# ReLU and row sum on one core: who clears the semaphores, how the last four rows are cut into loads, and which wait the last sum carries

## The chip, the cores and the metric

The kernel runs on 1 core of one Trainium2 chip. The metric is the device time of one execution in microseconds (us). On one core every run below was fast (granted clock 1.0 in each), so all of them can be compared. "Faster" and "slower" mean more than 2% with a 95% interval clear of it.

## The reference

```python
batch, seq, dim = 32, 512, 1024          # float32, normal random numbers
def reference(x):
    relu_x = np.maximum(x, 0)
    return np.sum(relu_x, axis=-1).astype(np.float32)
```

That is 16,384 rows of 1024 numbers: 67.11 MB in, 0.07 MB out, each byte read once.

## The kernel before

The rows lie over 128 partitions, 128 rows in each. Seven loads of 16 rows per partition (8 MB each) go through three buffers, and the last 16 rows come in shrinking loads. Most rows are clamped by ScalarE and summed by VectorE. Near the end each engine does whole rows alone, one instruction per row, whose accumulator then gives the sum. SyncE issues every load and store. Instruction order and semaphores are written by hand: each load has its own semaphore, which counts to 16 when it has landed (the trace has 16 increments of each); `act` and `dve` count finished instructions of ScalarE and VectorE; `stored` counts stores.

```python
TAIL = [8, 4, 2, 1]                  # rows per load at the end
PIECES = [244, 252, 260, 268]        # the last row, in four loads by columns
# ...
    for part, w in zip(parts, PIECES):
        arrived.append(load(part[:, :w], rows(m, 1)[:, 0, col : col + w]))
        col += w
    store(0, ROWS, *freed[0])
    store(ROWS, NT - ROWS - 2, n_act - 1, n_dve)

    last, w = parts[-1], PIECES[-1]
    for i in range(extra):           # the first three pieces; each sum becomes a column of the fourth
        dve_row(parts[i][:, :], last[:, w + i : w + i + 1], arrived[i])
    nc.vector.wait_ge(arrived[-1], 16)
    before_last = n_dve
    nc.vector.tensor_scalar(         # the last sum: 268 columns and three partial sums
        # ...
        accum_out=res[:, NT - 1 : NT],
    ).wait_op(sems.dve, before_last, "sem-ge").then_inc(sems.dve, 1)
    n_dve += 1
    store(NT - 2, 2, n_act, n_dve)   # the last store, two columns
    nc.sync.sem_inc(sems.issued, 1)
# ... and after the body:
    nc.sync.wait_ge(sems.stored, 16 * n_stores).then_inc(sems.stored, -16 * n_stores)
    # ...
    nc.gpsimd.wait_ge(sems.issued, 1)
    nc.gpsimd.drain(semaphore_range=cleared)
    nc.gpsimd.sem_clear(cleared)     # all semaphores back to 0 for the next execution
```

In the traces no instruction carries more than one wait (51 carry one in the kernel before). For the last sum, which needs two, one of them is an instruction of its own on VectorE's queue (21 ns).

Of the kernel before, what the change touches and what calls it, by code (L numbers as in the profile page):

```python
# [4 lines left out]
F32 = mybir.dt.float32  # L5
RELU = mybir.ActivationFunctionType.Relu
MAX, ADD = mybir.AluOpType.max, mybir.AluOpType.add
P = 128

ROWS = 16  # L10
# [3 lines left out]
TWO = [[16], [16], [16], [8, 8], [8, 8], [7, 7], []]  # L14
ACT = [0, 0, 0, 0, 0, 2, 9]
DVE = [0, 0, 0, 0, 0, 0, 7]

TAIL = [8, 4, 2, 1]
PIECES = [244, 252, 260, 268]

EARLY = 1

# [1 line left out]
def kernel(tc: tile.TileContext, x: bass.AP, out: bass.AP):  # L24
    nc = tc.nc
    sems = Semaphores(tc)

    tc.close()
    tc.compile()
    nc.cur_bb = nc.bb_map[tc.start_bb_name]  # L30
    body = nc.cur_bb.bb.instructions
    ends = list(body)
    body.clear()
    n_stores = relu_sum(nc, sems, x, out)
    body.extend(ends)


    nc.cur_bb = nc.bb_map[tc.start_bb_name + "_end"]
    nc.cur_bb.bb.instructions.clear()
    nc.sync.wait_ge(sems.stored, 16 * n_stores).then_inc(sems.stored, -16 * n_stores)  # L40
    nums = sorted(s.num for s in (*sems.loads, sems.act, sems.dve, sems.issued))
    cleared = range(nums[0], nums[-1] + 1)
    assert len(cleared) == len(nums)
    nc.gpsimd.wait_ge(sems.issued, 1)
    nc.gpsimd.drain(semaphore_range=cleared)
    nc.gpsimd.sem_clear(cleared)
    issue_ahead_of_the_barrier(tc, EARLY)


class Semaphores:  # L50
    def __init__(self, tc: tile.TileContext):
        n = len(TWO) + len(TAIL) + len(PIECES)
        self.loads = [tc.alloc_semaphore(f"load{i}") for i in range(n)]
        self.act = tc.alloc_semaphore("act")
        self.dve = tc.alloc_semaphore("dve")
        self.issued = tc.alloc_semaphore("issued")
        self.stored = tc.alloc_semaphore("stored")


def relu_sum(nc, sems: Semaphores, x: bass.AP, out: bass.AP):  # L60
    x_flat = x.flatten_outer_dims()
    N, D = x_flat.shape
    NT = N // P
    NB = len(TWO)
    assert N == P * NT == P * ROWS * (NB + 1)
    assert sum(TAIL) == ROWS - 1 and sum(PIECES) == D

    bufs = [nc.alloc_sbuf_tensor(f"io{i}", [P, ROWS, D], F32) for i in range(NBUF)]
    res = nc.alloc_sbuf_tensor("res", [P, NT], F32)
    extra = len(PIECES) - 1  # L70
    parts = [
        nc.alloc_sbuf_tensor(f"piece{i}", [P, w + extra * (i == extra)], F32)
        for i, w in enumerate(PIECES)
    ]


# [7 lines left out]
    def rows(m, n):  # L84
        if m < ROWS:
            return xf[:, m : m + n, :]
        return xv[:, m - ROWS : m - ROWS + n, :]

    def sums(m, n):
        if m < ROWS:  # L90
            return of[:, m : m + n], res[:, m : m + n]
        return ov[:, m - ROWS : m - ROWS + n], res[:, m : m + n]
# [3 lines left out]
    def load(dst, src, after=None):  # L96
        nonlocal n_load
        dma = nc.sync.dma_start(out=dst, in_=src)  # L98
        if after:
            dma.wait_op(sems.dve, after[1], "sem-ge")  # L100
        dma.then_inc(sems.loads[n_load], 16)
        n_load += 1
        return sems.loads[n_load - 1]

    def store(m, n, act, dve):
        nonlocal n_store
        dst, src = sums(m, n)
        nc.sync.wait_ge(sems.act, act)
        nc.sync.dma_start(out=dst, in_=src).wait_op(sems.dve, dve, "sem-ge").then_inc(
            sems.stored, 16  # L110
        )
        n_store += 1
# [16 lines left out]
    def act_row(ap, m, loaded):  # L129
        nonlocal n_act  # L130
        i = nc.scalar.activation(  # L131
            out=ap, in_=ap, func=RELU, accum_out=res[:, m : m + 1]
        )
        if loaded is not None:
            i.wait_op(loaded, 16, "sem-ge")
        i.then_inc(sems.act, 1)
        n_act += 1

    def dve_row(ap, accum_out, loaded):
        nonlocal n_dve  # L140
        i = nc.vector.tensor_scalar(  # L141
            out=ap,
            in0=ap,
            scalar1=0.0,
            scalar2=None,
            op0=MAX,
            op1=ADD,
            accum_out=accum_out,
        )
        if loaded is not None:  # L150
            i.wait_op(loaded, 16, "sem-ge")
        i.then_inc(sems.dve, 1)
        n_dve += 1

    freed = []
    m = 0
    for j in range(NB):
        buf = bufs[j % NBUF]
        loaded = load(buf[:, :, :], rows(m, ROWS), j >= NBUF and freed[j - NBUF])
        c = 0  # L160
# [19 lines left out]
    buf = bufs[NB % NBUF]  # L180
    c = 0
    for n in TAIL:
        loaded = load(
            buf[:, c : c + n, :], rows(m, n), None if c else freed[NB - NBUF]
        )
        for i in range(n):
# [3 lines left out]
                dve_row(buf[:, c, :], res[:, m : m + 1], loaded if i == 1 else None)  # L190
            c += 1
            m += 1
    col = 0
    arrived = []
    for part, w in zip(parts, PIECES):
        arrived.append(load(part[:, :w], rows(m, 1)[:, 0, col : col + w]))
        col += w



    store(0, ROWS, *freed[0])
    store(ROWS, NT - ROWS - 2, n_act - 1, n_dve)

    last, w = parts[-1], PIECES[-1]
    for i in range(extra):
        dve_row(parts[i][:, :], last[:, w + i : w + i + 1], arrived[i])
    nc.vector.wait_ge(arrived[-1], 16)
    before_last = n_dve
    nc.vector.tensor_scalar(  # L209
        out=last[:, :],  # L210
        in0=last[:, :],
# [1 line left out]
        scalar2=None,  # L213
        op0=MAX,
        op1=ADD,
        accum_out=res[:, NT - 1 : NT],
    ).wait_op(sems.dve, before_last, "sem-ge").then_inc(sems.dve, 1)
    n_dve += 1
    store(NT - 2, 2, n_act, n_dve)
    nc.sync.sem_inc(sems.issued, 1)  # L220
    return n_store


def issue_ahead_of_the_barrier(tc: tile.TileContext, n_loads: int):


    SP = mybir.EngineType.SP
    blocks = tc.nc.main_func.blocks
    opening = blocks[0].instructions
    body = next(b for b in blocks if b.name == tc.start_bb_name).instructions  # L230
    loads = [i for i in body if i.engine == SP][:n_loads]
    for i in loads:
        assert isinstance(i, mybir.InstDMACopy)
        body.remove(i)
    at = next(
        n
        for n, i in enumerate(opening)
        if i.engine == SP and isinstance(i, mybir.InstDrain)
    )
    opening[at:at] = loads  # L240
# [30 lines left out]
```

## Time and profile before

| | kernel before |
|---|---|
| time, median of 6 runs | 161.30 us (161.13 to 161.50) |
| span of the profiled run (first to last instruction) | 160.0 us |
| DMA queue, share of the span | 98.0% |
| VectorE, ScalarE busy | 74%, 65% |
| last load landed | 157.97 us |
| last sum, start to end | 158.11 to 158.55 us |
| end of the last store | 159.97 us |

The prediction below shows the lines for the queue, the chain that ended last and the last sums. Two more matter. In such lines DVE is VectorE, ACT is ScalarE, POOL is GpSimd and SP is SyncE; a q marks work of the engine's instruction queue, and L40 is line 40 of the kernel. The first is from the list of SyncE's waits (who waited for whom, us in total, times, longest); L40 is its wait for the stores:

```profile
SPq L40 <- SPq L40: 1.0, 1, 1.0
```

The second is GpSimd's clear of the semaphore range (duration in ns, least, median and most, then first and last start in us):

```profile
L46 POOLq EVENT_SEMAPHORE_RANGE_CLEAR  x1: 136/136/136, 159.1 to 159.1; - x1
```

It was over at 159.25, while SyncE stood waiting for the store until 159.99.

The stages of the tail are tenths of a microsecond. So I also use the trace's landing records (the moment at which the sixteenth count of a load's semaphore arrives) and its instruction starts, in thousandths of a microsecond.

### The profile page before, as it was taken

To read this page: it belongs to the slowest core of one execution; us is meant where nothing else is said; L and a number is where in the kernel's file an instruction comes from. 1 tells how busy PE (TensorE), PEld (TensorE's weight loads), DVE (VectorE), ACT (ScalarE), POOL (GpSimd) and SP (SyncE) were. 2 spreads that over 40 slices of the span, in tenths; PEclk is the share of its full clock that TensorE was granted. 3 is DMA by queue.
4 is the path that set the end of the run, shared out by engine and by line. 5 is a ranking of instruction groups with operands and counts; after the bars stand their busy time and mean duration, and the time that the engine had idled before them with its cause. 6 is when DMAs were issued, how large, how long until landed. Compare 5 with 4: busy or idle time off the path is not lost.

```text
span 160.0 us, 135 instructions
## 1 busy us (share of the span) xinstructions
DVE 117.7 (74%) x43; ACT 104.2 (65%) x50; POOL 0.2 (0%) x4
## 2 busy tenths in 40 slices
DVE  0000000009999499994999999999999999999995
ACT  3000049990699808996099951999339992499993
POOL 0000000000000000000000000000000000000000
DMA  7996996996996997999979969969969969898993
GB/s 262 524 508 279 524 492 295 524 491 295 524 491 295 524 442 344 524 393 393 524 344 442 524 262 524 524 262 524 524 262 524 491 295 524 377 410 385 428 405 109
DMA packets 2592, 67.18 MB, mean 420 GB/s; under 512 B 672, under 2 KB 1184, under 8 KB 1312
## 3 DMA queue, kind: packets, MB, share of 16 engines
q1 hardware_dynamic: 2592, 67.18, 98.0%
HBM read 67.11 MB, written 0.07 MB: 420 GB/s over the span
## 4 chain that ended last, share of the span: by engine, by line
DMA 43%; DVE 33%; ACT 17%; another core or an unknown queue 3%; SPq 1%; issue 0%
DVE res L124 32%; DMA io<-in_x_dram 25%; DMA piece<-in_x_dram 18%; ACT io L116 17%; SPq L98 1%; DVE piece L141 1%; DVE piece L209 0%
## 5 line engine op out<-in xcount | busy, mean ns | idle before, releaser
L124 DVE TENSOR_REDUCE res<-io 128x8 f32<-128x8192 f32 (+2 forms) x9 | 101.1, 11291 | 40.2 <-ACT io L116 40.2
L116 ACT ACTIVATE io<-io 128x8192 f32<-128x8192 f32 (+2 forms) x9 | 81.7, 9111 | 47.2 <-DMA io<-in_x_dram 47.2
L131 ACT ACTIVATE io<-io 128x1024 f32<-128x1024 f32 x20 | 20.9, 1045 | 5.4 <-DMA io<-in_x_dram 5.3
L141 DVE TENSOR_SCALAR_CACHE_REDUCE io<-io 128x1024 f32<-128x1024 f32 x13 | 15.1, 1225 | 0.2
L131 ACT ACTIVATION_READ_ACCUMULATOR io<-io 128x1 f32 x20 | 3.7, 187 | 0.0
L116 ACT ACT_TABLE_LOAD x1 | 1.3, 1283 | 0.8 <-PEq L255 0.8
L141 DVE TENSOR_SCALAR_CACHE_REDUCE piece<-piece 128x244 f32<-128x244 f32 (+2 forms) x3 | 1.2, 415 | 0.5 <-DMA piece<-in_x_dram 0.5
L141 DVE DVE_READ_ACCUMULATOR io<-io 128x1 f32 x13 | 1.2, 93 | 0.0
L209 DVE TENSOR_SCALAR_CACHE_REDUCE piece<-piece 128x271 f32<-128x271 f32 x1 | 0.4, 435 | 0.0
L141 DVE DVE_READ_ACCUMULATOR piece<-piece 128x1 f32 x3 | 0.2, 83 | 0.0
L255 POOL MEMSET const-bfloat16-1.0<- 128x1 bf16 x1 | 0.1, 103 | 0.0
L255 POOL MEMSET const-uint8-127<- 128x1 uint8 x1 | 0.1, 103 | 0.0
L255 POOL MEMSET const-float32-1.0<- 128x1 f32 x1 | 0.1, 100 | 0.0
L255 POOL MEMSET const-float32-0.0<- 128x1 f32 x1 | 0.1, 99 | 0.2 <-issue 0.2
L209 DVE DVE_READ_ACCUMULATOR piece<-piece 128x1 f32 x1 | 0.1, 82 | 0.0
## 6 DMA issues: line engine op xcount, KB each, us to landing
io<-in_x_dram SPq DMA_DIRECT2D x1, 4096.0 KB, 21.6
io<-in_x_dram SPq DMA_DIRECT2D x1, 2048.0 KB, 26.1
io<-in_x_dram SPq DMA_DIRECT2D x1, 1024.0 KB, 28.1
io<-in_x_dram SPq DMA_DIRECT2D x1, 512.0 KB, 28.9
piece<-in_x_dram SPq DMA_DIRECT2D x1, 134.0 KB, 28.4
piece<-in_x_dram SPq DMA_DIRECT2D x1, 130.0 KB, 28.6
piece<-in_x_dram SPq DMA_DIRECT2D x1, 126.0 KB, 28.7
piece<-in_x_dram SPq DMA_DIRECT2D x1, 122.0 KB, 28.8
```

What stands on the lines that cost most here:

```text
L98: dma = nc.sync.dma_start(out=dst, in_=src)
L116: i = nc.scalar.activation(out=ap, in_=ap, func=RELU)
L124: nc.vector.tensor_reduce(out=res[:, m : m + n], in_=ap, axis=mybir.AxisListType.X, op=ADD).wait_op(sems.act, n_act, "sem-ge").then_inc(se ...
L131: i = nc.scalar.activation(out=ap, in_=ap, func=RELU, accum_out=res[:, m : m + 1])
L141: i = nc.vector.tensor_scalar(out=ap, in0=ap, scalar1=0.0, scalar2=None, op0=MAX, op1=ADD, accum_out=accum_out,)
L209: nc.vector.tensor_scalar(out=last[:, :], in0=last[:, :], scalar1=0.0, scalar2=None, op0=MAX, op1=ADD, accum_out=res[:, NT - 1 : NT],).wai ...
L255: nc = _bacc.Bacc("TRN2", target_bir_lowering=False, num_devices=1)
```

## The change

There are three parts. (1) SyncE clears the semaphores between issuing the last store and waiting for it, and GpSimd is left out. (2) The last four rows come in four loads instead of six: two rows and 360 columns of the third; the fourth row, now for ScalarE; and the rest of the third in 260 and 404 columns. (3) The last sum carries the wait for its load, and the separate wait is the one for VectorE's own earlier sums.

```diff
-TAIL = [8, 4, 2, 1]
-PIECES = [244, 252, 260, 268]
+TAIL = [8, 4]
+PIECES = [360, 260, 404]
@@
-    nc.sync.wait_ge(sems.stored, 16 * n_stores).then_inc(sems.stored, -16 * n_stores)
...
-    nc.gpsimd.wait_ge(sems.issued, 1)
-    nc.gpsimd.drain(semaphore_range=cleared)
-    nc.gpsimd.sem_clear(cleared)
+    nc.sync.sem_clear(cleared)
+    nc.sync.wait_ge(sems.stored, 16 * n_stores).then_inc(sems.stored, -16 * n_stores)
@@
+    first = PIECES[0]
+    loaded = load(
+        buf[:, :, :].rearrange("p c d -> p (c d)")[:, c * D : (c + 2) * D + first],
+        rows(m, 3).rearrange("p c d -> p (c d)")[:, : 2 * D + first],
+    )
+    act_row(buf[:, c, :], m, loaded)
+    dve_row(buf[:, c + 1, :], res[:, m + 1 : m + 2], loaded)
+    last_loaded = load(buf[:, c + 3, :], rows(m + 3, 1)[:, 0, :])
... (the loads of 260 and 404 columns)
+    sums_done = n_act, n_dve
+    act_row(buf[:, c + 3, :], m + 3, last_loaded)
@@
-    for i in range(extra):
-        dve_row(parts[i][:, :], last[:, w + i : w + i + 1], arrived[i])
-    nc.vector.wait_ge(arrived[-1], 16)
+    dve_row(buf[:, c + 2, :first], last[:, w : w + 1], None)
+    for i in range(1, extra):
+        dve_row(parts[i - 1][:, :], last[:, w + i : w + i + 1], arrived[i - 1])
+    nc.vector.wait_ge(sems.dve, n_dve)
...
-    ).wait_op(sems.dve, before_last, "sem-ge").then_inc(sems.dve, 1)
+    ).wait_op(arrived[-1], 16, "sem-ge").then_inc(sems.dve, 1)
```

More of the change, by code (lines that the diff above doesn't have):

```diff
@@ L39 @@
     nc.cur_bb.bb.instructions.clear()
-    nc.sync.wait_ge(sems.stored, 16 * n_stores).then_inc(sems.stored, -16 * n_stores)
-    nums = sorted(s.num for s in (*sems.loads, sems.act, sems.dve, sems.issued))
+    nums = sorted(s.num for s in (*sems.loads, sems.act, sems.dve))
     cleared = range(nums[0], nums[-1] + 1)
     assert len(cleared) == len(nums)
-    nc.gpsimd.wait_ge(sems.issued, 1)
-    nc.gpsimd.drain(semaphore_range=cleared)
-    nc.gpsimd.sem_clear(cleared)
+    nc.sync.sem_clear(cleared)
+    nc.sync.wait_ge(sems.stored, 16 * n_stores).then_inc(sems.stored, -16 * n_stores)
     issue_ahead_of_the_barrier(tc, EARLY)
@@ L51, in __init__ @@
     def __init__(self, tc: tile.TileContext):
-        n = len(TWO) + len(TAIL) + len(PIECES)
+        n = len(TWO) + len(TAIL) + 1 + len(PIECES)
         self.loads = [tc.alloc_semaphore(f"load{i}") for i in range(n)]
@@ L55, in __init__ @@
         self.dve = tc.alloc_semaphore("dve")
-        self.issued = tc.alloc_semaphore("issued")
         self.stored = tc.alloc_semaphore("stored")
@@ L65, in relu_sum @@
     assert N == P * NT == P * ROWS * (NB + 1)
-    assert sum(TAIL) == ROWS - 1 and sum(PIECES) == D
+    assert sum(TAIL) == ROWS - 4 and sum(PIECES) == D
     bufs = [nc.alloc_sbuf_tensor(f"io{i}", [P, ROWS, D], F32) for i in range(NBUF)]
@@ L71, in relu_sum @@
     parts = [
-        nc.alloc_sbuf_tensor(f"piece{i}", [P, w + extra * (i == extra)], F32)
-        for i, w in enumerate(PIECES)
+        nc.alloc_sbuf_tensor(f"piece{i + 1}", [P, w + extra * (i + 1 == extra)], F32)
+        for i, w in enumerate(PIECES[1:])
     ]
@@ L192, in relu_sum @@
             m += 1
-    col = 0
+    first = PIECES[0]
[6 more added lines that the diff above has]
+    last_loaded = load(buf[:, c + 3, :], rows(m + 3, 1)[:, 0, :])
     arrived = []
-    for part, w in zip(parts, PIECES):
-        arrived.append(load(part[:, :w], rows(m, 1)[:, 0, col : col + w]))
+    col = first
+    for part, w in zip(parts, PIECES[1:]):
+        arrived.append(load(part[:, :w], rows(m + 2, 1)[:, 0, col : col + w]))
         col += w
+    sums_done = n_act, n_dve
+    act_row(buf[:, c + 3, :], m + 3, last_loaded)
     store(0, ROWS, *freed[0])
-    store(ROWS, NT - ROWS - 2, n_act - 1, n_dve)
+    store(ROWS, NT - ROWS - 2, *sums_done)
     last, w = parts[-1], PIECES[-1]
-    for i in range(extra):
-        dve_row(parts[i][:, :], last[:, w + i : w + i + 1], arrived[i])
-    nc.vector.wait_ge(arrived[-1], 16)
-    before_last = n_dve
+    dve_row(buf[:, c + 2, :first], last[:, w : w + 1], None)
+    for i in range(1, extra):
+        dve_row(parts[i - 1][:, :], last[:, w + i : w + i + 1], arrived[i - 1])
+    nc.vector.wait_ge(sems.dve, n_dve)
     nc.vector.tensor_scalar(
@@ L215, in relu_sum @@
         op1=ADD,
-        accum_out=res[:, NT - 1 : NT],
-    ).wait_op(sems.dve, before_last, "sem-ge").then_inc(sems.dve, 1)
+        accum_out=res[:, NT - 2 : NT - 1],
+    ).wait_op(arrived[-1], 16, "sem-ge").then_inc(sems.dve, 1)
     n_dve += 1
     store(NT - 2, 2, n_act, n_dve)
-    nc.sync.sem_inc(sems.issued, 1)
     return n_store
```

## The prediction

> **What bounds the kernel now.** I read the page of the kernel before from the top: engine shares, DMA queue, the chain that ended last, and the DMA issues; then the timeline of VectorE and ScalarE over the last 5 us; then the list of instructions of the small tiles called piece. Engine shares and the queue come first:
>
> ```profile
> DVE 117.7 (74%) x43; ACT 104.2 (65%) x50; POOL 0.2 (0%) x4
> ...
> q1 hardware_dynamic: 2592, 67.18, 98.0%
> HBM read 67.11 MB, written 0.07 MB: 420 GB/s over the span
> ```
>
> No engine is full, but the queue's packets fill 98% of the span of 160.0 us. The input is 67.11 MB, read once, and the change reads the same bytes. So the middle of the kernel can't move, and I asked only about the two ends. The front is untouched. The back end is in the last steps of the chain and in the landing times:
>
> ```profile
> 128.06 28.83 DMA piece<-in_x_dram
> 156.89 0.03 issue
> 156.91 1.17 DVE piece L141 x6
> 158.09 0.02 issue
> 158.11 0.44 DVE piece L209 x2
> ```
>
> ```profile
> io<-in_x_dram SPq DMA_DIRECT2D x1, 2048.0 KB, 26.1
> io<-in_x_dram SPq DMA_DIRECT2D x1, 1024.0 KB, 28.1
> io<-in_x_dram SPq DMA_DIRECT2D x1, 512.0 KB, 28.9
> piece<-in_x_dram SPq DMA_DIRECT2D x1, 134.0 KB, 28.4
> ```
>
> The chain starts its last stretch at the landing of the FIRST piece (156.89), then has VectorE work through four pieces without a stop until 158.55. But is VectorE truly late, or does it just keep pace with the landings? Issue time plus time to landing gives the landings. The 1024 KB load was issued at 127.10, so it landed at 155.2. The row of 512 KB: 127.57 + 28.9 = 156.5. The pieces, issued at 128.06, 128.55, 129.06 and 129.6, landed at 156.9, 157.25, 157.65 and 158.0 (28.8, 28.7, 28.6, 28.4 after issue). So the fourth piece came at about 158.0 while VectorE was on the third:
>
> ```profile
> 157.65 0.42 DVE L141 TENSOR_SCALAR_CACHE_REDUCE piece<-piece 128x260 f32<-128x260 f32 x1
> 158.00 0.08 DVE L141 DVE_READ_ACCUMULATOR piece<-piece 128x1 f32 x1
> 158.11 0.43 DVE L209 TENSOR_SCALAR_CACHE_REDUCE piece<-piece 128x271 f32<-128x271 f32 x1
> 158.47 0.08 DVE L209 DVE_READ_ACCUMULATOR piece<-piece 128x1 f32 x1
> ```
>
> VectorE was free at 158.08 and began the last sum at 158.11. The last data and VectorE are level to within 0.1 us; this tail is already balanced. After 158.55 only the store of the last two sums is left. It was issued at 158.58 and landed 1.4 us later (the out_dram issue of 1.0 KB), which is the end of the span.
>
> [...] the five last loads land in the order of issue. So I may add up the load times one after another. [...] Here the 1.0 KB store still takes 1.4 us[...], and this is the cover for the semaphore clearing. [...] 244 columns take 407 ns and 1024 take 1223 ns, which is 1.05 ns a column and about 150 ns that does not shrink. [...]
>
> **The change, part by part.**
>
> 1. *SyncE clears the semaphores.* Removed: GpSimd's wait, its drain (88 ns in the trace, at 158.99) and its clear (136 ns at 159.11, over at 159.25), and SyncE's increment that released it. All end 0.75 us before SyncE's last wait is met (159.99). Added: one clear on SyncE, between issuing the last store and waiting for it. SyncE stands in that wait from about 158.97 to 159.99 (the chain of waits lists 1.0 us for it). At GpSimd's 136 ns, or even at five times that, it fits. Worth on the path: 0.
>
> 2. *The last four rows in four loads.* Before: 1024 KB (two rows), 512 KB, then 122, 126, 130 and 134 KB. After: 1204 KB (rows 12 and 13, and 360 columns of row 14), 512 KB (row 15, now for ScalarE), 130 KB and 202 KB. Same bytes, two loads fewer. What do two small loads cost? The 512 KB in one load took 156.5 - 155.2 = 1.3 us; the 512 KB in four pieces took 158.0 - 156.5 = 1.5 us. So four pieces cost some 0.2 us more than one load, about 0.05 each over the plain rate. The new landings, as an estimate: 1204 KB at the 2.48 us that 1024 KB took (152.7 to 155.2) needs 2.92, so 155.64; row 15 at +1.3, so 156.94; 130 KB at +0.37 (a piece's step), so 157.31; 202 KB at +0.51, so 157.82. The last data is 0.15 us earlier than 157.97.
>
> 3. *VectorE's tail.* Row 13 starts at 155.67 and the next sum can start 1.15 later (the step between 1024-column sums in the timeline): 156.82. The 360 columns need no wait (same load): 407 ns + 116 x 1.05 = 0.53 us, next start 0.04 before its end: 157.31. Piece of 260: landed 157.31, so it runs from 157.34, and its accumulator read ends 0.43 later, at 157.77. The last sum, 404 + 2 columns, waits for its load at 157.82 and for VectorE, ready at 157.80 to 157.88 with the separate semaphore instruction: start 157.86. It costs 407 + 162 x 1.05 = 577 ns, about 0.14 more than the 435 ns of today's; end 158.45. Today it is 158.55. **Gain 0.10 us**: 0.15 from the landing and about 0.10 from waiting in its own instruction and a later start no longer behind VectorE, less 0.14 for the longer last sum.
>
> 4. *ScalarE.* Row 15 lands at 156.94 and a row takes 1.06 + 0.19 with 0.09 overlap (156.53 to 157.68 today), so it ends near 158.12, before VectorE's 158.45. It does not set the end. The large second store loses its wait for the last ScalarE row and goes at about 156.95, later than today's 156.49 because rows 12 and 13 land later; it is still issued over 1 us ahead of the last store.
>
> Sum: the last store goes at 158.48 instead of 158.58, +1.4 us: a span of about 159.9, against 160.0. 161.31 - 0.1 = 161.2.
>
> **The rivals.**
>
> *The clear was holding the end.* If GpSimd's path set the end of the execution outside the span, taking it away could give up to its length, some 0.3 us (158.95 to 159.25). For: the measured time is 1.3 us longer than the span, and no profile shows what lies there. Against: SyncE's wait ended 0.75 us after GpSimd. It would give about 160.9.
>
> *The clear becomes the end.* If SyncE needed over 1 us to clear the range it would push the last wait; the 136 ns on GpSimd speaks against it, but no record shows it on SyncE. It would give 161.5 or more.
>
> *The longer last sum isn't paid for.* If the last piece lands as late as today (157.97), because bytes and not the number of loads set it, the last sum ends at 157.99 + 0.58 = 158.57, and the time is 161.3, no gain.
>
> *ScalarE becomes the bound.* Row 15 landing 0.35 us later than I say would be needed; the same bytes lie ahead of it, so I give it little.
>
> **Range and chances.** A verdict of 2% needs 3.2 us. The whole stretch from the last landing to the end is 2.0 us, of which 1.4 is the store's flight, and the rest of the kernel is the same reads on a 98% full queue. So within 2% is nearly certain. The three runs before span 161.17 to 161.5, wider than my gain; the rivals reach from 160.9 to 161.5. I say 161.2, and 160.8 to 161.6 for the range.
>
> **What would show it right or wrong.** In the profile of the changed kernel: still 98% on the queue; the last piece landing about 0.15 us earlier, counted from where the 2048 KB load landed; the last sum beginning within 0.05 us of that landing (if it begins later, VectorE is the limit and step 3 is wrong); the last sum at about 0.58 us; the store again 1.4 us; SyncE's clear between that store's issue and its wait, and that wait shorter by the clear's time with the same end. It is wrong if the clear moves the end, if the landings of the last loads don't move, or if an earlier stretch of the DMA queue has gaps that it does not have now.

161.31 us, the median of the three runs of the kernel before that it had, less 0.1 us of tail, comes to 161.2.

## The result, and the profile after

| | before | after |
|---|---|---|
| time, median of 6 runs each | 161.30 us | 161.23 us (161.09 to 161.38) |
| ratio, 95% interval | | 0.9996 (0.9984 to 1.0009): same |
| span of the profiled run | 160.0 us | 159.8 us |

A ratio is the mean time of one kernel's fast runs over that of the other's of the same rounds, so not quite the ratio of the medians. The outputs are correct.

From the page of the changed kernel, engine shares and queue:

```profile
DVE 117.5 (74%) x41; ACT 104.2 (65%) x50; POOL 0.2 (0%) x4
...
q1 hardware_dynamic: 2304, 67.18, 98.0%
```

There are fewer packets (2304, where it was 2592) for the same 67.18 MB, and the queue is as full as before: the seven 8 MB loads land 19.3 to 19.4 us apart in both profiles. The DMA issues of the last loads (KB, then us from issue to landing):

```profile
io<-in_x_dram SPq DMA_DIRECT2D x1, 1204.0 KB, 28.6
io<-in_x_dram SPq DMA_DIRECT2D x1, 512.0 KB, 29.4
piece<-in_x_dram SPq DMA_DIRECT2D x1, 202.0 KB, 29.3
piece<-in_x_dram SPq DMA_DIRECT2D x1, 130.0 KB, 29.3
```

The chain that ended last (start us, us, what), from where it leaves the loads:

```profile
126.93 28.56 DMA io<-in_x_dram
155.49 0.02 issue
155.51 1.68 DVE io L140 x4
157.19 0.44 DVE piece L140 x2
157.63 0.03 issue
157.66 0.02 DVEq L218
157.68 0.07 issue
157.75 0.58 DVE piece L219 x2
```

Read it upward. The last sum (L219) was released by L218, the separate wait on VectorE's queue, and that one by VectorE's own sum of the 260 columns. The printed chain joins the loads only at 155.49, the landing of the 1204 KB load.

The landing records show a later joint, which the chain doesn't print. The 130 KB load landed at 157.167, and the sum of its 260 columns began 0.023 us later, at 157.190. VectorE could have begun it some 0.08 us sooner, at 157.108, with the accumulator read of the sum before it: the 360-column sum, which has no wait, began together with the accumulator read before it (both at 156.660), and in e8 a sum whose wait was already met did the same (both at 157.175). The 0.08 us is an estimate from these starts. So the last load does not set the end, but the load before it does: from its landing on, VectorE does the 260-column sum, stands 0.130 us in the separate wait, and does the last sum.

The timeline shows the rest (start us, us, engine, line, operation):

```profile
157.54 0.08 DVE L140 DVE_READ_ACCUMULATOR piece<-piece 128x1 f32 x1
157.75 0.58 DVE L219 TENSOR_SCALAR_CACHE_REDUCE piece<-piece 128x406 f32<-128x406 f32 x1
157.77 0.19 ACT L130 ACTIVATION_READ_ACCUMULATOR io<-io 128x1 f32 x1
158.25 0.08 DVE L219 DVE_READ_ACCUMULATOR piece<-piece 128x1 f32 x1
158.37 0.33 SPq L108 DMA_DIRECT2D out_dram<-res  x1
```

ScalarE is done at 157.96, before VectorE at 158.34. Then SyncE's clear and its wait:

```profile
L45 SPq EVENT_SEMAPHORE_RANGE_CLEAR  x1: 58/58/58, 158.7 to 158.7; - x1
...
SPq L46 <- SPq L46: 1.0, 1, 1.0
```

**Where did 0.2 us of span come from?** Mostly not from the change. The very first 8 MB load, which the change does not touch, landed at 22.02 us before and at 21.87 after, and the 2048 KB load of the tail at 152.73 and 152.56. So 0.17 us of the difference was there before the first changed load. The fair measure of the change is the time *from the landing of the 2048 KB load*:

| from the landing of the 2048 KB load, us | before | after |
|---|---|---|
| last load landed | 5.24 | 5.11 |
| last sum starts | 5.39 | 5.20 |
| last sum ends | 5.83 | 5.78 |

The gain is 0.05 us in this pair of profiles. Counted from the last landing it has three terms. The landing is 0.13 us earlier. The start follows the landing by 0.084 instead of 0.145, a gain of 0.06. The last sum is 0.14 longer, because it has 406 columns instead of 271.

That is bookkeeping, and not cause, since in both kernels the last sum waits for VectorE and not for the last load. VectorE's chain starts at the landing of the last load but one. In the kernel before that is the 130 KB piece, at 4.90 us after the 2048 KB landing (its sum began 0.024 after it); in the changed kernel it is the 130 KB load, at 4.61 (202 KB come behind it, where it was 134 KB). So the causes are: 0.29 us from that earlier landing, less 0.10 for the separate wait (0.130 after VectorE's own sum, where it was 0.035), less 0.14 for the longer last sum. Six profiles with the changed loads and waits (this one, e0, e4, e5, e6, e10) bear it out. The end of the last sum follows the 130 KB landing by 1.167 to 1.170 us, a spread of 0.003; it follows the last landing by 0.649 to 0.668, a spread of 0.019. No run moved that landing on purpose.

### The profile page after: what moved, and what is told of

Its sections match the earlier page's. It is cut to its first block, busy times and chain, and to the rows that moved or that the text cites. A ratio compares the mean times of both kernels' runs of the same rounds, so it can differ in the third digit from the quotient of the medians.

```text
span 159.8 us, 129 instructions
## 1 busy us (share of the span) xinstructions
DVE 117.5 (74%) x41; ACT 104.2 (65%) x50; POOL 0.2 (0%) x4
## 2 busy tenths in 40 slices
DMA packets 2304, 67.18 MB, mean 420 GB/s; under 512 B 640, under 2 KB 896, under 8 KB 1024
## 3 DMA queue, kind: packets, MB, share of 16 engines
q1 hardware_dynamic: 2304, 67.18, 98.0%
## 4 chain that ended last, share of the span: by engine, by line
DMA 43%; DVE 34%; ACT 17%; another core or an unknown queue 3%; SPq 0%; issue 0%; DVEq 0%
DMA io<-in_x_dram 43%; DVE res L123 32%; ACT io L115 17%; DVE io L140 1%; SPq L97 0%; DVE piece L219 0%; DVE piece L140 0%; DVEq L218 0%
## 5 line engine op out<-in xcount | busy, mean ns | idle before, releaser
L140 DVE TENSOR_SCALAR_CACHE_REDUCE io<-io 128x1024 f32<-128x1024 f32 (+1 forms) x14 | 15.5, 1165 | 0.7 <-DMA io<-in_x_dram 0.6
L219 DVE TENSOR_SCALAR_CACHE_REDUCE piece<-piece 128x406 f32<-128x406 f32 x1 | 0.6, 576 | 0.1
L219 DVE DVE_READ_ACCUMULATOR piece<-piece 128x1 f32 x1 | 0.1, 83 | 0.0
```

Source lines behind the costliest of these rows:

```text
L140: i = nc.vector.tensor_scalar(out=ap, in0=ap, scalar1=0.0, scalar2=None, op0=MAX, op1=ADD, accum_out=accum_out,)
L219: nc.vector.tensor_scalar(out=last[:, :], in0=last[:, :], scalar1=0.0, scalar2=None, op0=MAX, op1=ADD, accum_out=res[:, NT - 2 : NT - 1],) ...
```

## The experiments

Eleven runs were made: the changed kernel twice more, and nine kernels made for a question. All gave the right output. The diffs below are cut to the lines that matter. "Tail" below is the time from the landing of the 2048 KB load to the end of the last sum.

**The theory:** the change only rearranges the last 6 us of a kernel whose DMA queue (98.0% full) sets the rest; the clear is hidden either way; and the tail gains some 0.05 us. **The rivals:** the clear was on the path outside the span; the span's 0.2 us is the change's doing; the order of the waits costs nothing, or helps always; the end is set by the last load and not by VectorE.

### The changed kernel again: e0 and e10

No edit. 

> The changed kernel once more, for a second profile and more timed runs. Theory (the tail is worth some 0.05 us): ratio to the kernel before 0.999 to 1.000, and the interval holds 1. In its profile the time from the landing of the 2048 KB load to the end of the last sum is 5.78 us, as in the first profile (5.83 in the kernel before), while the landing of the 2048 KB load itself may differ by 0.2 us from run to run. Rival (the 0.2 us by which the first two profiles differ in span is the change's doing): the span is again 0.2 us under that of the kernel before.

Measured: median 161.17 us, ratio 0.9988 (0.9976 to 1.0000). The tail is 5.76 us, the last landing 5.10.

> The changed kernel beside the one without the separate wait, on the same chip. Both theories: ratio to the kernel before 0.9985 to 1.0000; end of the last sum 5.76 to 5.78 us after the landing of the 2048 KB load, the last sum's start 0.08 us after the last landing.

Measured on another chip: 161.22 us, ratio 1.0000 (0.9986 to 1.0014), tail 5.76, last sum 0.070 after the landing. All three ratios hold with a gain of 0.05 to 0.07 us (0.9996 to 0.9997), and none of them resolves it. (Put together, the 16 runs of the changed kernel have a median of 161.22 and the 26 of the kernel before, from the same rounds, 161.28. That leans the same way as the tail, but it mixes chips and rounds and is no test.) Three more kernels below have the same tail as the changed one (e4, e5, e6): 5.76, 5.75 and 5.77. The landing of the 2048 KB load ran from 152.44 to 152.82 over all thirteen profiles, with no order by kernel: e4, with the changed kernel's loads, has the earliest and e5, with the same loads, the latest. The landings drift by more than the change is worth. The 0.2 us of span do come back in e0, so that rival isn't excluded by e0 alone. It is excluded by the tail clock, and by e5: up to its clears it is the changed kernel, and its 2048 KB load landed at 152.82, 0.09 later than in the kernel before.

### One part at a time: e1, e2, e3

```diff
 e1: the kernel before, with part 1 alone
-    nc.gpsimd.wait_ge(sems.issued, 1)
-    nc.gpsimd.drain(semaphore_range=cleared)
-    nc.gpsimd.sem_clear(cleared)
+    nc.sync.sem_clear(cleared)          # ahead of the wait for the stores
```

> The kernel before, with only the clearing moved to SyncE. Theory (the clearing lies beside the last store's flight): ratio 1.000 within 0.001; in the profile the clear takes about 60 ns on SyncE right after the last store's issue, and the end of the last sum and the store's 1.4 us are as before. Rival (GpSimd's path held the end outside the span): 0.3 us faster, ratio 0.998.

Measured: 161.30 us, ratio 0.9994 (0.9982 to 1.0007); tail 5.85. The clear took 63 ns at 158.80, and the store landed at 159.82. Moving the clear gave nothing that the runs can see. The interval ends at 0.9982, and the rival's 0.3 us would be 0.9981, so this run alone excludes it only by a hair. Time less span (the spans to 0.1 us) is 1.31 to 1.42 us in the runs of the kernel before, 1.33 to 1.41 in e1 and 1.32 to 1.42 in the three sets of the changed kernel. Nothing like 0.3 us outside the span went away.

```diff
 e2: the kernel before, with part 2 alone (the new loads; old clear, old order of waits)
-    nc.vector.wait_ge(sems.dve, n_dve)
+    nc.vector.wait_ge(arrived[-1], 16)
...
-    ).wait_op(arrived[-1], 16, "sem-ge")
+    ).wait_op(sems.dve, before_last, "sem-ge")
```

(This diff is against the changed kernel; GpSimd's clear is put back as well.)

> The kernel before, with only the new loads of the last four rows; GpSimd clears, and the last sum keeps the old order of its two waits (a separate wait for the load, then its own for VectorE). Theory: ratio 0.999 to 1.000. From the landing of the 2048 KB load, the last load lands after 5.11 us (5.24 before), and the last sum starts about 0.12 us after that landing, where it was 0.084 with the new order: the separate wait passes 0.03 after the landing and an instruction behind it needs 0.09 more. End of the last sum 5.82 us after the 2048 KB landing. Rival (the order of the waits costs nothing): the last sum starts 0.03 us after the landing.

Measured: 161.27 us, ratio 0.9992 (0.9980 to 1.0005). The last load landed after 5.08 us, and the last sum began 0.120 after it, as expected. The tail is 5.79. The chain of e2, last steps:

```profile
157.90 0.03 issue
157.92 0.02 DVEq L221
157.94 0.07 issue
158.02 0.58 DVE piece L223 x2
```

Now the separate wait (L221) is for the load, landed at 157.896, and the sum still starts 0.09 us behind the wait.

```diff
 e3: the kernel before, with part 3 alone
-    nc.vector.wait_ge(arrived[-1], 16)
+    nc.vector.wait_ge(sems.dve, n_dve)
...
-    ).wait_op(sems.dve, before_last, "sem-ge")
+    ).wait_op(arrived[-1], 16, "sem-ge")
```

> The kernel before, with only the order of the last sum's two waits turned round (a separate wait for VectorE's own count, then the load in the sum's own instruction). Theory: here VectorE comes last, 0.11 us after the load, so the new order is the wrong way round: the last sum starts 0.13 us after the end of the accumulator read before it, where it was 0.035, and the tail is 0.09 us longer: ratio 1.0006, not to be told from 1 in the times, but plain in the profile. Rival (waiting in the own instruction is quicker whatever comes last): the last sum starts earlier than before, within 0.03 us.

Measured: 161.32 us, ratio 1.0000 (0.9987 to 1.0012), tail 5.95: the longest of all with the old loads, by 0.10 to 0.12. The chain of e3, last steps:

```profile
157.90 0.03 issue
157.93 0.02 DVEq L207
157.95 0.07 issue
158.02 0.44 DVE piece L208 x2
```

VectorE's sum before it ended at 157.891, and the last sum began 0.131 later, where in the kernel before it began 0.035 later. So the separate wait cost about 0.1 us here, where the thing it waits for comes last. In the old tail VectorE comes last (in the kernel before, 0.11 us after the load), and there part 3 alone is a loss. It is of use only together with part 2, and there it is worth little: the tail of e2, without it, is 5.79, and of the changed kernel 5.75 to 5.78.

### The clear, multiplied and moved: e4, e5, e6

```diff
 e4 (8 times), e5 (40 times), against the changed kernel
-    nc.sync.sem_clear(cleared)
+    for _ in range(8):                  # 40
+        nc.sync.sem_clear(cleared)
```

> The changed kernel with SyncE's clear written eight times. Theory (the clear lies in the 1.03 us between the last store's issue and its landing): one clear takes 0.06 us and, with some 0.04 us to the next instruction, eight take 0.8 us, which still fits: the end of SyncE's wait does not move and the ratio to the kernel before stays 0.999. Rival (a clear on SyncE is paid on the path): +0.4 to +0.8 us, ratio 1.003 to 1.005.

> The changed kernel with SyncE's clear written forty times, to overrun the cover on purpose. Theory: 40 clears at 0.06 to 0.10 us are 2.4 to 4.0 us, the cover is 1.03, so the end comes 1.4 to 3.0 us later: ratio 1.008 to 1.018. If it does not move at all, the cover is not what hides the clear.

Measured: e4 161.14 us, ratio 0.9990 (0.9976 to 1.0003); e5 163.35 us, ratio 1.0126 (1.0113 to 1.0140). SyncE's clears and its wait in e4:

```profile
L46 SPq EVENT_SEMAPHORE_RANGE_CLEAR  x8: 48/48/58, 158.6 to 159.2; - x8
...
SPq L47 <- SPq L47: 0.4, 1, 0.4
```

Seven clears more took 0.6 us out of the wait (1.0 to 0.4) and nothing out of the end. In e5 the clears step at 0.078 us and run from 158.97 to 162.09. The store had landed at 160.00, so the end comes 2.1 us after it, in agreement with the 2.05 us by which the median is longer. The cover is real, about 1 us, and one clear uses 6% of it.

```diff
 e6: the changed kernel, the clear behind the wait
+    nc.sync.wait_ge(sems.stored, 16 * n_stores).then_inc(sems.stored, -16 * n_stores)
     nc.sync.sem_clear(cleared)
-    nc.sync.wait_ge(sems.stored, 16 * n_stores).then_inc(sems.stored, -16 * n_stores)
```

> The changed kernel with SyncE's clear behind its wait for the stores instead of ahead of it. Theory: now the clear's 0.06 us and the step to it, 0.04, lie on the path: the span is 0.1 us longer from the store's issue to the last instruction (1.42 us in the changed kernel, 1.52 here), ratio to the kernel before 0.9995 to 1.0005, too little for the times alone. Rival (the position is of no account): 1.42 us as before.

Measured: 161.37 us, ratio 0.9999 (0.9986 to 1.0013). In the trace the store was issued at 158.476 and the last instruction ended at 160.029: 1.55 us, against 1.44 from 158.365 to 159.807 in the changed kernel. (The 1.42 and 1.52 expected were taken to the start of the last instruction.) The position is worth 0.11 us, about as expected, but the times alone don't show it.

### One more sum on VectorE: e7

```diff
 e7: the changed kernel
     nc.vector.wait_ge(sems.dve, n_dve)
+    scratch = nc.alloc_sbuf_tensor("scratch", [P, 1], F32)
+    dve_row(buf[:, c + 1, :], scratch[:, :], None)
```

> The changed kernel with one more sum of 1024 columns on VectorE, ahead of the last sum and behind its separate wait (its result goes to a tile of its own, the output stays right). Theory (VectorE's tail behind the last load is on the path, one for one): the end of the last sum and the time move by the step of such a sum, 1.15 us: ratio 1.006 to 1.007 to the kernel before. Rival (the end is set by the last load or by something outside the span): less than half of that.

Measured: 162.20 us, ratio 1.0053 (1.0039 to 1.0067); tail 6.82, so 1.05 us longer than the changed kernel's 5.76 to 5.78. What VectorE does behind its sum of the 260 columns is on the path one for one (1.15 us more work and 0.1 us less of a wait). The 0.1 us short of the expected 1.15 is explained by the chain of e7:

```profile
157.23 0.44 DVE piece L140 x2
157.67 0.02 issue
157.70 1.23 DVE io L140 x2
158.92 0.50 DVE piece L221 x2
```

There is no separate wait in it: the added sum has no wait of its own in the kernel's text, and I take it that it took over the one ahead of it. It begins 0.035 us after the sum before it, where the changed kernel's last sum begins 0.130 after. The added sum cost 1.15, and a separate wait of about 0.1 went away.

### The last row in eight pieces: e8

```diff
 e8: the kernel before
-PIECES = [244, 252, 260, 268]
+PIECES = [128] * 8
```

> The kernel before with its last row in eight pieces of 128 columns instead of four. Theory (a small load costs some 0.05 us over the plain rate, on the queue): the row's landings stretch from 1.46 us (four pieces) to about 1.65 from the landing of the 512 KB load. VectorE then needs eight sums of some 0.25 us, step by step, and is level with or behind the loads, so the end of the last sum comes 0.3 to 0.6 us later counted from the 2048 KB landing (5.83 us before). Rival (the bytes alone set the landings): 1.3 to 1.46 us for the row whatever the pieces.

Measured: 161.76 us, ratio 1.0030 (1.0013 to 1.0047). The row's landings took 1.66 us (four pieces 1.46; a whole row of 512 KB in one load 1.29). So each load more costs the queue about 0.05 to 0.06 us (1.66 less 1.46 over four loads, 1.46 less 1.29 over three), about as the prediction worked out, and the rival is wrong. What the cost hangs on stays open: each load more also brings 144 packets (3168 on the page here, 2592 before, over four loads) and makes the row's packets smaller, and no run has one without the other. But the tail is 5.99, only 0.16 longer than before, and not the 0.3 to 0.6 that I wrote: the pieces land about 0.2 us apart, and VectorE's sums of 128 columns step at 0.21, not 0.25, so VectorE nearly keeps up. The median is 0.49 us longer than the kernel before, which the tail does not explain. Time less span is 1.59 to 1.70 us here, against 1.33 to 1.42 in the kernel before in the same rounds. Some 0.3 us lie outside the span, and no record shows on what. This stays open. The changed kernel shows no such thing: its time less span is that of the kernel before.

### No separate wait at all: e9

```diff
 e9: the changed kernel; the 260-column sum counts up the last load's semaphore
-    nc.vector.wait_ge(sems.dve, n_dve)
...
-    ).wait_op(arrived[-1], 16, "sem-ge")
+    ).wait_op(arrived[-1], 17, "sem-ge")
```

> The changed kernel without the separate wait: the sum of the 260-column piece counts up the last load's semaphore, and the last sum waits in its own instruction for 17, which is 16 from the load and 1 from that sum. Theory (the separate wait costs 0.13 us after VectorE's own sum, where a wait in the instruction costs 0.035, and 0.025 after a landing): the last sum starts 0.03 us after the last landing, where it was 0.08, and ends some 5.71 us after the landing of the 2048 KB load (5.78 and 5.76 in the changed kernel); 0.05 us, too little for the times. Rival (the separate wait is not what holds the last sum, VectorE or the load is): the start stays 0.08 us after the landing.

Measured: 161.22 us, ratio 1.0001 (0.9988 to 1.0013), beside e10's 1.0000 in the same rounds. The tail is 5.71 us, and the last sum begins 0.023 after the landing at 157.763. The chain of e9:

```profile
155.62 1.68 DVE io L140 x4
157.30 0.47 DVE piece L140 x2
157.76 0.02 issue
157.79 0.58 DVE piece L222 x2
```

So in the changed kernel the separate wait held the last sum back by 0.05 us; without it the last load's own landing sets the start. This version has the shortest tail of all, by 0.05 us, and the times don't see it. There is no version here that beats the kernel before by something the runs can tell.

## Why the prediction was right

It said 161.2 us and "same"; the median is 161.23. That the median fell so near is partly luck: six runs of one kernel scatter over 0.3 us, three times the gain that was said. Its steps, one by one, with the tail clock:

- **The bound.** Right: the queue fills 98.0% of the span before and after, and only the tail moved.
- **The clear is worth 0.** Right, and the rivals fall: e1 shows no gain, e4 shows room for eight clears, and e5 shows the end move once the room is used up. The clear took 58 ns on SyncE, less than the 136 of GpSimd. One sign did not come: SyncE's wait was to be shorter by the clear's time, and it is 0.99 us where it was 1.02, since the increment that released GpSimd (17 ns, at 158.952) went away too.
- **The landings.** Right to 0.02 us. From the 2048 KB load the prediction had 2.92 us to the 1204 KB load, then 1.30, 0.37 and 0.51; measured are 2.93, 1.30, 0.38 and 0.50. The last landing gained 0.13 us, where 0.15 was said. The rival "bytes alone set the landings" falls by that, and by e8.
- **VectorE's tail.** Right up to the last sum: from the 1204 KB landing to the end of the 260-column sum 2.13 us, predicted and measured. The length of the last sum is right as well (577 ns said, 576 measured). The term that was mis-sized is the separate wait: the prediction let VectorE be ready 0.03 to 0.11 us after its own sum, and the last sum began 0.130 after it. By the prediction's own test (a start over 0.05 us after the landing means that VectorE is the limit) the changed kernel is held by VectorE and its separate wait, with 0.084, and step 3 is wrong in that term. So the tail gained 0.05 us in the first pair (0.05 to 0.10 over all profiles with either tail, 0.07 by their means), where 0.10 was said. The prediction's account of the gain is off as well. It has the 260-column sum start at its own landing, which is right, but then counts the last landing as the source. Measured are 0.29 from the landing of the load before the last, less 0.10 for the separate wait, less 0.14 for the longer sum. Its reading of the kernel before, four pieces "without a stop", hides the same thing: each of the first three sums began 0.024 or 0.025 us after its own landing.
- **Part 3 as a gain.** The prediction counted waiting in the own instruction among the gains. That holds only with the new loads. There the load lands 0.046 us after VectorE's own sum has ended (157.622 and 157.668), and with the old order (e2) the start is 0.120 after the landing instead of 0.084. In the old tail it is a loss of 0.1 us (e3).
- **ScalarE.** It ended at 157.96, before VectorE, as said.
- **The span.** 159.9 was said and 159.8 measured. The difference is mostly not a merit of the change: the queue ran 0.15 us earlier from the first load on, and 0.17 by the 2048 KB load.

The stretch that the change can touch is a few microseconds of 161, so 3.2 us could not come out of it.

## What to carry to other kernels

Before shaving a tail, measure from the last event that the change does not touch; from the start of the span, drift in the loads (0.4 us here) hides or fakes a gain of 0.05. When an instruction needs two waits, as the last sum here, put the one that comes LAST into the instruction and the one that is met first ahead of it. The wrong way round cost the last sum 0.1 us in e3 and some 0.04 in e2. Which one is last changes with the data's arrival (VectorE 0.11 us after the load in the kernel before, the load 0.046 us after VectorE in the changed kernel), so look at both times in the trace. Ask also which load the engine's last stretch of work starts from: here it was not the last one. Housekeeping in the flight of the last store was free here as long as it fitted into the 1.0 us that SyncE waits (e4's eight clears fit, e5's forty at 0.078 us do not): take it away for simplicity, but expect no time for it.

## Prices measured here

- **A separate wait ahead of an instruction.** After VectorE's own sum: 0.13 us with a separate wait (e3, and the changed kernel), 0.035 with the wait in the instruction (the kernel before) or with no separate wait in the chain (e7). After a landing: 0.120 (e2) and 0.023 to 0.025 (e9, and the kernel before).
- **Clearing a range of semaphores.** 48 to 63 ns on SyncE (15 or 17 semaphores), with a step of 0.08 us when repeated (e4, e5), and on GpSimd 118 ns for 16 semaphores (e2), 136 for 18 (the kernel before, e3) and 158 for 22 (e8).
- **One load more in the full queue.** About 0.05 to 0.06 us, an estimate from the landings of e8 and of the kernel before. A store of 1.0 KB, issued from SyncE, took 1.4 us from issue to landing (DMA issues of the kernel before, the changed kernel, e0, e1, e2 and e6).
- **The max-and-sum with an accumulator on VectorE.** In the kernel before it took 407 ns for 244 columns and 1223 for 1024 (mean of six): 816 ns over 780 columns, so by estimate 1.05 ns a column and about 150 ns that does not shrink. This line gives 576 for 406 columns against 571 to 577 measured in these runs, 528 against 522 to 524 for 360, and 286 against 279 to 286 for 128 (e8). The 1024 columns themselves took 1207 to 1227. The accumulator read of 80 to 97 ns comes on top, and overlaps by 0.07 to 0.09 us.
